# The causal mask of the diagonal attention blocks: an add into the kept row F on GpSimd and VectorE in place of small TensorE matmuls

## The chip, the cores and the metric

The kernel runs on one core of a Trainium2 chip. The metric is the device time of one execution in microseconds (us), as the median of several runs. A core has five engines that each work through their own instructions in order and wait for one another through semaphores: TensorE (PE in the profile; its weight loads are PEld), VectorE (DVE), ScalarE (ACT), GpSimd (POOL) and SyncE (SP, here a DMA queue). "SBUF" is the on-chip memory of 128 partitions, "PSUM" the accumulator memory that TensorE writes.

## What is computed

One decoder layer on 1024 tokens of width 1024: RMSNorm, one combined projection, a Mamba-2 (SSD) branch, a forgetting-attention branch (16 heads of 64), a gated merge, an output projection, and a post-norm with the residual. The change is in the attention branch alone:

```python
log_f = jax.nn.log_sigmoid(f_raw + fgate_b)        # one forget gate per head and token
fcum  = jnp.cumsum(log_f, axis=-1)                 # F
for blk in range(seqlen // 128):                   # 8 query blocks of 128
    s = q[q0:q1] @ k[:q1].T * scale + fcum[q0:q1, None] - fcum[None, :q1]
    s = jnp.where(kpos[None, :] <= qpos[:, None], s, -inf)
    o = softmax(s) @ v[:q1]
```

The mask matters only in the 128 x 128 square where a query block meets its own keys. Everything to the left of that square is allowed, and nothing to the right of it is computed.

## The kernel before

**The stages.** All large projections go through one stream of Strassen-like products (`Stream`, `Pair`), each a run of 12 matmuls of 128 x 512 in fp32r in two halves of 6 (`matmuls`, called through `mm`, L130). Their weights are split into a high and a low part by ScalarE (`wop<-raw` or `wop<-sum`, L351) and VectorE (L352). Their results leave PSUM through ScalarE (`s<-pb`, L404; `th<-pb`, L412) and VectorE (L414 to L418). From 0 to about 688 us this stream runs beside the SSD branch, from 688 to 1140 us beside attention, and after that alone.

**Attention.** Two heads are worked at a time, one on partitions 0 to 63 and one on 64 to 127, which makes 8 head pairs (`hp`). A pair has six groups, numbered here by `m` = 6 `hp` + `g` from 0 to 47. `GROUPS` (query blocks, half of the keys) is ((7,6),1), ((7,6),0), ((5,4),1), ((5,4),0), ((3,2),0), ((1,0),0). Within a group, `u` = 0 is the first named block and `u` = 1 the second. Groups g = 0, 2, 4 and 5 hold a diagonal square for both blocks, g = 1 and 3 hold none. So there are 32 groups with diagonal squares and 64 diagonal blocks for a pair of heads. The widths of the keys are 512 and 384 in g = 0 and 4, and 256 and 128 in g = 2 and 5.

**One group**, in program order:

- `scores`: for `u` = 0 and then 1, six fp32r matmuls (`s<-k,q`) and, in a diagonal block, four small bf16 matmuls (`s<-far,eye`) that add the mask into the last 128 columns. Then for each head VectorE adds the row F (tile `fb`, which is F of all keys, spread over 128 partitions) and takes the minimum (`ex<-s,fb`, L1464, a custom operation with a second instruction that reads its accumulator into `nm`), and ScalarE takes the exponential in place (`ex<-ex,nm`, L1468). A group so has four of each.
- `fill(m, 0)`: a planned share of matmuls of the stream, to keep TensorE at work while VectorE and ScalarE make the exponentials.
- `turned`: TensorE transposes the exponentials (`pt<-ident,ex`, L133). In even `m` other than 0 a small transpose of `ns` goes first, and the bank of the last key block, where only `u` = 0 takes part. The bank after that takes both heads of `u` = 0 and then both heads of `u` = 1. ScalarE, and for one bank VectorE, copies the banks out (`p<-pt`, L1499, L1497); ScalarE also sends a normalizer (`st<-pt`, L1391).
- `fill(m, 1)`, and then, at the start of the next round, `weighted`: the products with v (`av<-p,v`).

**What sets the order.** TensorE's order is that of the program (`keep_in_program_order`). So is that of everything wrapped in `pin`. The other instructions of VectorE, ScalarE, GpSimd and SyncE are ordered by the compiler's own scheduler, which may put an instruction of the stream between two of attention's. What each engine executes is then a fixed list.

**The mask before.** `eye` holds two shifted unit matrices and `far` the value 1e30 above the diagonal. For each head the two matmuls `eye` x `far` (64 rows each) add 1e30 where a key is later than the query. The sign is turned in the exponential (scale -1), so that 1e30 gives 0.

**Other users of the queues.** GpSimd carries the differences of the SSD operands (`less`, L213) with their stores (`t_s`, `t_a`, L195), the stores of attention's result (`ya_dram`, L1530) and of `ms_dram` (L1061), and in the last pair the sums of weights (L357, L373). SyncE issues nearly all loads, those of `fb` (L1333) among them: half 1 of the next pair in g = 2, half 0 in g = 5.

Of the kernel before, what the change touches and what calls it, by code (L numbers as in the profile page):

```python
# [16 lines left out]
P = 128  # L17
# [69 lines left out]
def hybrid_layer(ctx: ExitStack, tc, a, out):  # L87
# [41 lines left out]
    def mm(*args, **kw):  # L129
        return tc.keep_in_program_order(nc.tensor.matmul(*args, **kw))  # L130
# [7 lines left out]
    def small(name="th"):  # L138
        return gp.tile([P, HALF], F32, tag="th", name=name)
# [1153 lines left out]
    with tc.tile_pool(name="att", bufs=1, reuse_waits="tile", side="right") as ap, tc.tile_pool(  # L1293
# [1 line left out]
    ) as pp:  # L1295
        rows = [slice(64 * e, 64 * e + 64) for e in range(2)]

        eye = ap.tile([P, 192], BF16, name="eye")
        far = ap.tile([P, 192], BF16, name="far")
        nc.vector.memset(eye, 0.0)  # L1300
        big, beyond = small("big"), small("beyond")
        nc.vector.memset(big[:, 0:192], -NEG)
        for e in range(2):
            nc.vector.tensor_copy(eye[rows[e], 64:P], ident[rows[e], rows[e]])
            nc.gpsimd.affine_select(
                beyond[:, 192 * e : 192 * e + 192], big[:, 0:192], [[1, 192]], ALU.is_gt, 0.0, base=64 * e - 64,
                channel_multiplier=-1,
            )
            nc.vector.tensor_copy(far[rows[e], :], beyond[rows[e], 192 * e : 192 * e + 192])

        corner = [(eye[:, 64:192], far[:, 64:192]), (eye[:, 0:P], far[:, 0:P])]

# [123 lines left out]
        def scores(hp, g, u):  # L1436

            pair, h = GROUPS[g]
            i = pair[u]
            w = min(HALF, (i + 1) * P - h * HALF)  # L1440
            s = [pp.tile([P, HALF], F32, tag="s", bufs=4, name="s") for e in range(2)]
            t, keys = q[hp, pair], k[hp, h]
            isl = slice(i % 2 * P, i % 2 * P + P)
            ops = [(t[:, x, isl], keys[:, y, 0:w]) for x, y in ((0, 0), (0, 1), (1, 0))]
            diagonal = h == i // 4
            for m, (x, y) in enumerate(ops):
                for e in range(2):
                    mm(
                        s[e][:, 0:w], x[rows[e]], y[rows[e]], start=(m == 0), stop=(m == 2 and not diagonal),
                        skip_group_check=True,  # L1450
                    )
            if diagonal:
                for n, (x, y) in enumerate(corner):
                    for e in range(2):
                        mm(
                            s[e][:, w - P : w], x[rows[e]], y[rows[e]], start=False, stop=(n == 1),
                            skip_group_check=True,
                        )
            hd = heads[hp]
            for e in range(2):  # L1460
                o = ex[:, e, u, 0:w]
                nm = hd.at(hd.nm, i, h, e)
                pin(
                    nc.vector.tensor_tensor_reduce(  # L1464
                        o, s[e][:, 0:w], fb[hp, h][:, e, 0:w], 1.0, 3.0e38, ALU.add, ALU.min, nm
                    )
                )
                pin(nc.scalar.activation(o, o, AF.Exp, scale=-1.0, bias=nm, accum_out=hd.at(hd.sm, i, h, e)))  # L1468
# [258 lines left out]
```

## Time and profile before

| | us |
|---|---|
| median of 3 runs | 1303.09 (1302.53 to 1304.8) |
| the profiled execution | 1300.96 |
| its span, first to last instruction | 1299.3 |
| TensorE busy | 1256.0 |
| VectorE busy | 1005.9 |
| ScalarE busy | 792.0 |
| GpSimd busy | 262.0 |

The profile is of one execution. It gives each engine's instructions with start and duration, and for idle time before an instruction what ended it. The granted TensorE clock is 0.997 of full speed on average. Times below are us from the start of the span. In a row of a timeline the first number is the start, the second how long the row's instructions took together, and "xN" how many instructions of one kind are merged in it.

### The profile page before, as it was taken

Reading aid. Unit: us, or ns where it says so; the run is one execution under the profiler, and the core shown is the slowest. Engines: PE = TensorE matmul, PEld = TensorE weight load, DVE = VectorE, ACT = ScalarE, POOL = GpSimd, SP = SyncE. Lnnn points to the kernel's source line nnn. Section 1 sums busy time; section 2 is a strip of 40 time slices with the busy share of each in tenths; the row PEclk is TensorE's granted clock in tenths of the full one; section 3 lists DMA queues with packets and bytes.
Section 4 is the critical chain, followed back from the end, with each engine's and each line's share of the span. In section 5 each row is a group of like instructions: output and inputs, shape, how many; then the busy total and the mean of one; then the engine's idle time right before and its main releaser. Section 6 shows DMA issues by size and latency. Waiting matters only on the chain.

```text
span 1299.3 us, 20943 instructions
## 1 busy us (share of the span) xinstructions
PE 1256.0 (97%) x7054; PEld 984.4 (76%) x7054; DVE 1005.9 (77%) x1994; ACT 792.0 (61%) x1738; POOL 262.0 (20%) x250
## 2 busy tenths in 40 slices
PE   5999999999999999999999999999999999899997
PEld 4678778887888888878877777777667777678886
DVE  7989886987888888898676666666787677686975
ACT  7745665566665665566546566566775566653754
POOL 3000440012400340124001121120001001146052
PEclk9999999999999999999999999999999999999999
DMA  8233542645436543655375575666866658556932
GB/s 295 76 107 76 159 146 87 201 145 180 127 120 200 182 131 98 211 167 145 98 229 189 181 232 187 220 222 205 284 225 224 224 184 292 192 181 196 361 112 99
DMA packets 153515, 233.57 MB, mean 180 GB/s; under 512 B 15968, under 2 KB 61504, under 8 KB 153408
## 3 DMA queue, kind: packets, MB, share of 16 engines
q1 hardware_dynamic: 137408, 197.14, 47.7%
q10 hardware_dynamic: 11136, 19.11, 3.9%
q0 software_dynamic: 4864, 15.99, 3.2%
q8 instruction: 55, 0.90, 0.3%
q14 instruction: 52, 0.43, 0.1%
HBM read 162.99 MB, written 72.34 MB: 181 GB/s over the span
## 4 chain that ended last, share of the span: by engine, by line
PE 67%; DVE 12%; ACT 8%; DMA 7%; issue 4%; SPq 1%; POOL 0%; ACTq 0%; DVEq 0%; POOLq 0%
PE pb L130 28%; PE pc L130 15%; PE pd L130 5%; PE av L130 4%; PE pt L133 4%; PE s L130 4%; ACT ex L1468 3%; PE yps L130 2%; DVE wop L352 2%; ACT wop L351 1%; DVE sum L357 1%; DVE xs L771 1%; DVE ex L1464 1%; PE tr L133 1%; DMA xt<-in_x 1%
## 5 line engine op out<-in xcount | busy, mean ns | idle before, releaser
L1468 ACT ACTIVATE ex<-ex,nm 128x512 f32<-128x512 f32 (+1 forms) x192 | 116.0, 606 | 127.9 <-DVE nm L1464 127.8
L352 DVE TENSOR_TENSOR wop<-sum,wop 128x512 fp32r<-128x512 f32 x180 | 136.6, 760 | 56.4 <-ACT wop L351 54.8
L351 ACT ACTIVATE wop<-sum 128x512 fp32r<-128x512 f32 x180 | 112.3, 625 | 84.5 <-DVE sum L357 37.9
L404 ACT ACTIVATE s<-pb 128x512 f32<-128x512 f32 x144 | 85.1, 591 | 94.1 <-PE pb L130 90.9
L352 DVE TENSOR_TENSOR wop<-raw,wop 128x512 fp32r<-128x512 f32 x144 | 102.1, 710 | 45.2 <-ACT wop L351 43.9
L130 PE MATMUL pc<-x3h,wop 128*128 128x512 f32 x384 | 130.5, 397 | 1.7 <-DVE th L414 1.3
L130 PE MATMUL pb<-x0h,wop 128*128 128x512 f32 x384 | 131.2, 398 | 0.0
L130 PE MATMUL pb<-x5h,wop 128*128 128x512 f32 x384 | 129.3, 396 | 1.2 <-ACT s L404 1.2
L130 PE MATMUL pb<-x6h,wop 128*128 128x512 f32 x384 | 129.2, 395 | 1.3 <-ACT s L404 1.3
L130 PE MATMUL pc<-x2h,wop 128*128 128x512 f32 x384 | 130.2, 398 | 0.0
L130 PE MATMUL pb<-x4h,wop 128*128 128x512 f32 x384 | 129.4, 395 | 0.0
L1464 DVE CUSTOM_DVE_ANT_0 ex<-s,fb 128x512 f32<-128x512 f32 (+1 forms) x192 | 95.7, 552 | 34.1 <-PE s L130 34.0
L351 ACT ACTIVATE wop<-raw 128x512 fp32r<-128x512 f32 x144 | 89.6, 623 | 13.9 <-PE pd L130 6.1
L130 PE MATMUL pd<-x1h,wop 128*128 128x512 f32 x288 | 96.3, 394 | 0.0
L130 PEld LDWEIGHTS pc<-x3h,wop 128*128 128x128 f32 x384 | 72.4, 189 | 19.4 <-DVE th L414 1.7
L130 PEld LDWEIGHTS pb<-x5h,wop 128*128 128x128 f32 x384 | 72.1, 188 | 18.8 <-ACT s L404 2.3
L130 PEld LDWEIGHTS pb<-x6h,wop 128*128 128x128 f32 x384 | 72.2, 188 | 17.6 <-ACT s L404 1.7
L130 PEld LDWEIGHTS pc<-x2h,wop 128*128 128x128 f32 x384 | 72.1, 188 | 17.0 <-issue 1.4
L130 PEld LDWEIGHTS pb<-x0h,wop 128*128 128x128 f32 x384 | 72.7, 189 | 16.1 <-issue 0.9
L130 PEld LDWEIGHTS pb<-x4h,wop 128*128 128x128 f32 x384 | 72.1, 188 | 16.1 <-issue 0.9
L133 PE MATMUL pt<-ident,ex 128*128 128x128 f32 x576 | 77.2, 277 | 7.2 <-ACT ex L1468 6.7
L133 PEld LDWEIGHTS pt<-ident,ex 128*128 128x128 f32 x576 | 65.9, 142 | 19.4 <-ACT ex L1468 13.5
(310 smaller groups left out, 2918.8 us busy)
## 6 DMA issues: line engine op xcount, KB each, us to landing
raw<-in_wu SPq DMA_DIRECT2D x128, 256.0 KB
csb<-cs_dram SPq DMA_DIRECT2D x32, 256.0 KB
fb<-f_dram SPq DMA_DIRECT2D x16, 512.0 KB
rb<-st_dram SPq DMA_DIRECT2D x48, 128.0 KB
wd<-in_wo SPq DMA_DIRECT2D x40, 128.0 KB
xt<-in_x SPq DMA_DIRECT2D x8, 512.0 KB
gs_dram<-th ACTq DMA_DIRECT2D x16, 256.0 KB
qh_dram<-th ACTq DMA_DIRECT2D x16, 256.0 KB
```

What stands on the lines that cost most here:

```text
L130: return tc.keep_in_program_order(nc.tensor.matmul(*args, **kw))
L133: return tc.keep_in_program_order(nc.tensor.transpose(out_, in_, idn))
L351: nc.scalar.activation(op[:, 0], src, AF.Copy)
L352: nc.vector.tensor_tensor(op[:, 1], src, op[:, 0], ALU.subtract)
L357: self.adds.tensor_tensor(t, x, y, ALU.add)
L404: nc.scalar.activation(s, ps, AF.Copy)
L771: nc.vector.scalar_tensor_tensor(d, u[:, o + j : o + j + HALF], cw[:, tile_idx, j : j + 1], d, ALU.mult, ALU.add)
L1464: nc.vector.tensor_tensor_reduce(o, s[e][:, 0:w], fb[hp, h][:, e, 0:w], 1.0, 3.0e38, ALU.add, ALU.min, nm)
L1468: pin(nc.scalar.activation(o, o, AF.Exp, scale=-1.0, bias=nm, accum_out=hd.at(hd.sm, i, h, e)))
```

## The change

`eye`, `far` and the four small matmuls of each diagonal block are gone. One tile `beyond` (128 x 128, fp32) holds 1e30 above the diagonal. Before a diagonal block is reduced on VectorE, `beyond` is added in place to the 128 columns of `fb` that belong to its square, for both heads in one instruction (128 x 2 x 128). Columns of `fb` are masked only after the last block that needs them unmasked, so each of these adds also waits for earlier readers. Of the eight blocks of a head pair the odd ones (7, 5, 3, 1) are masked by GpSimd, a group or more ahead, and the even ones (6, 4, 2, 0, which are `u` = 1) by VectorE, between the two reductions of `u` = 0 and the two of `u` = 1. That makes 32 adds on GpSimd and 32 on VectorE; 256 matmuls and their 256 weight loads leave TensorE. The adds are pinned, so that they keep their place among the other pinned instructions of their engine.

```diff
-        eye = ap.tile([P, 192], BF16, name="eye")
-        far = ap.tile([P, 192], BF16, name="far")
...
-        corner = [(eye[:, 64:192], far[:, 64:192]), (eye[:, 0:P], far[:, 0:P])]
+        beyond = ap.tile([P, P], F32, name="beyond")
+        big = small("big")
+        nc.vector.memset(big[:, 0:P], -NEG)
+        nc.gpsimd.affine_select(beyond, big[:, 0:P], [[1, P]], ALU.is_gt, 0.0, base=0, channel_multiplier=-1)
...
+        def corner(hp, i, engine):
+
+            f = fb[hp, i // 4][:, :, i % 4 * P : i % 4 * P + P]
+            pin(engine.tensor_tensor(f, f, beyond.unsqueeze(1).to_broadcast([P, 2, P]), ALU.add))
...
             for m, (x, y) in enumerate(ops):
                 for e in range(2):
                     mm(
-                        s[e][:, 0:w], x[rows[e]], y[rows[e]], start=(m == 0), stop=(m == 2 and not diagonal),
-                        skip_group_check=True,
+                        s[e][:, 0:w], x[rows[e]], y[rows[e]], start=(m == 0), stop=(m == 2), skip_group_check=True,
                     )
-            if diagonal:
-                for n, (x, y) in enumerate(corner):
-                    for e in range(2):
-                        mm(
-                            s[e][:, w - P : w], x[rows[e]], y[rows[e]], start=False, stop=(n == 1),
-                            skip_group_check=True,
-                        )
             hd = heads[hp]
+            if u and h == i // 4:
+                corner(hp, i, nc.vector)
...
             hp, g = divmod(m, 6)
             more = hp + 1 < NK
+            if g in (1, 3, 4):
+                corner(hp, {1: 5, 3: 3, 4: 1}[g], nc.gpsimd)
+            if g == 4 and more:
+                corner(hp + 1, 7, nc.gpsimd)
...
+        corner(0, 7, nc.gpsimd)
```

More of the change, by code (lines that the diff above doesn't have):

```diff
@@ L1296, in hybrid_layer @@
         rows = [slice(64 * e, 64 * e + 64) for e in range(2)]
-        eye = ap.tile([P, 192], BF16, name="eye")
-        far = ap.tile([P, 192], BF16, name="far")
-        nc.vector.memset(eye, 0.0)
-        big, beyond = small("big"), small("beyond")
-        nc.vector.memset(big[:, 0:192], -NEG)
-        for e in range(2):
[L1304 to L1307, printed above, removed]
-            )
-            nc.vector.tensor_copy(far[rows[e], :], beyond[rows[e], 192 * e : 192 * e + 192])
-        corner = [(eye[:, 64:192], far[:, 64:192]), (eye[:, 0:P], far[:, 0:P])]
+        beyond = ap.tile([P, P], F32, name="beyond")
+        big = small("big")
+        nc.vector.memset(big[:, 0:P], -NEG)
+        nc.gpsimd.affine_select(beyond, big[:, 0:P], [[1, P]], ALU.is_gt, 0.0, base=0, channel_multiplier=-1)
         GROUPS = [((7, 6), 1), ((7, 6), 0), ((5, 4), 1), ((5, 4), 0), ((3, 2), 0), ((1, 0), 0)]
@@ L1444, in scores @@
             ops = [(t[:, x, isl], keys[:, y, 0:w]) for x, y in ((0, 0), (0, 1), (1, 0))]
-            diagonal = h == i // 4
             for m, (x, y) in enumerate(ops):
@@ L1448, in scores @@
                     mm(
-                        s[e][:, 0:w], x[rows[e]], y[rows[e]], start=(m == 0), stop=(m == 2 and not diagonal),
-                        skip_group_check=True,
-                    )
-            if diagonal:
-                for n, (x, y) in enumerate(corner):
-                    for e in range(2):
-                        mm(
-                            s[e][:, w - P : w], x[rows[e]], y[rows[e]], start=False, stop=(n == 1),
-                            skip_group_check=True,
-                        )
+                        s[e][:, 0:w], x[rows[e]], y[rows[e]], start=(m == 0), stop=(m == 2), skip_group_check=True,
+                    )
             hd = heads[hp]
+            if u and h == i // 4:
+                corner(hp, i, nc.vector)
             for e in range(2):
```

## The prediction

> **What bounds the kernel now.** I read the page's busy times and its chain first, then the table of stages, then TensorE's waits in the attention stage (688 to 1140 us), where the whole change lies.
>
> ```profile
> PE 1256.0 (97%) x7054; PEld 984.4 (76%) x7054; DVE 1005.9 (77%) x1994; ACT 792.0 (61%) x1738; POOL 262.0 (20%) x250
> ...
> PE 67%; DVE 12%; ACT 8%; DMA 7%; issue 4%; SPq 1%; POOL 0%; ACTq 0%; DVEq 0%; POOLq 0%
> ```
> ```profile
> 688.00:910.00 222.00, 221.21 (x1499) 168.63 (x1499) 147.34 (x398) 138.52 (x351) 36.09 (x41) 1.00 0.62 201
> 910.00:1140.00 230.00, 218.69 (x1508) 159.35 (x1506) 171.41 (x458) 151.24 (x394) 23.91 (x38) 0.99 0.68 229
> ```
> ```profile
> PE pt L133 <- ACT ex L1468: 6.7, 17, 1.3
> PE av L130 <- ACT p L1499: 4.5, 8, 1.2
> ```
>
> Until 910 us (pairs 0 to 3) TensorE is busy 221.21 of 222.00 us: an instruction taken from it there is time gained, if nothing else becomes late. From 910 to 1140 it idles 11.3 of 230 us, and those gaps name ScalarE: transposes wait for exponentials (6.7 us in 17 waits), products with v for copies (4.5 us in 8). There the chain scores, VectorE's reduction, ScalarE's exponential, transpose has no cover left.
>
> **What TensorE gets back.** One group with diagonal squares (pair 4, widths 512 and 384), and the next one, without:
>
> ```profile
> 919.34 0.98 PE L130 MATMUL s<-k,q 64*128 64x512 f32 x6
> 920.16 0.29 PE L130 MATMUL s<-far,eye 64*128 64x128 bf16 x4
> 920.26 0.77 PE L130 MATMUL s<-k,q 64*128 64x384 f32 x6
> 920.87 0.28 PE L130 MATMUL s<-far,eye 64*128 64x128 bf16 x4
> 921.09 0.50 PE L130 MATMUL pb<-x5h,wop 128*128 128x512 f32 x1
> ```
> ```profile
> 930.51 1.67 PE L130 MATMUL s<-k,q 64*128 64x512 f32 x12
> 932.11 0.50 PE L130 MATMUL pc<-x3h,wop 128*128 128x512 f32 x1
> ```
>
> Matmuls overlap, so I go by starts. The mask delays what follows it by 0.10 us in block `u` = 0 (920.16 to 920.26) and by 0.22 in `u` = 1 (920.87 to 921.09), of which some 0.1 is the switch to full-width matmuls that stays: at least 0.22 a group. From above: the unmasked group takes 1.60 us from first score to fill, the masked one 1.75, though its second block is narrower by 0.82 - 0.61 = 0.21: at most 0.36. I take **0.27**, inside both, for all 32 groups: 8.6 us (7.0 to 11.5) if every group of TensorE's queue became that much shorter. The compiled order shows TensorE's list otherwise unchanged, 512 entries fewer, so that the change does what it says there.
>
> It counts only where ScalarE is ready for an earlier TensorE. By the table below, 18 of the 32 groups have that: **18 x 0.27 = 4.9 us gained**.
>
> **What VectorE gets.** An add on two SBUF operands, 128 x 256 in all, between the reductions of `u` = 0 and `u` = 1. It must wait for the last reader of its columns, and the next reduction for it, both on VectorE itself.
>
> ```profile
> L1430 DVE TENSOR_TENSOR zr<-o 128x256 f32<-128x256 f32 x16 | 7.8, 487 | 0.1
> ```
> ```profile
> 915.58 0.20 DVE L1373 RECIPROCAL sm<-sm 128x8 f32<-128x8 f32 x1 [1.16 <-ACT ex L1468]
> 915.82 0.17 DVE L1374 TENSOR_SCALAR ns<-sm 128x8 f32<-128x8 f32 x1
> ...
> 923.40 0.69 DVE L1464 CUSTOM_DVE_ANT_0 ex<-s,fb 128x512 f32<-128x512 f32 x1
> 924.01 0.08 DVE L1464 DVE_READ_ACCUMULATOR2_ANT nm<- 128x1 f32 x1
> 924.01 0.55 DVE L1464 CUSTOM_DVE_ANT_0 ex<-s,fb 128x384 f32<-128x384 f32 x1
> ```
>
> Independent reductions overlap by 0.08 us (923.40 + 0.69 against 924.01). A dependent instruction starts 0.04 after the end of the one before (915.78, 915.82). So an add costs 0.12 + 0.49 + 0.04 = about 0.6 us, 19 us in 32. VectorE is 66 to 75% busy in these stages, and ScalarE, with exponentials 0.70 us apart, hides more than half: the third exponential of this group would be ready 0.3 us later than now. That alone costs little (below nothing too: the scores of `u` = 0 end 0.1 us earlier).
>
> **What the scheduler does with it.** This is the larger part. It now expects the exponentials of `u` = 1 late and puts stream work before them. In 14 groups, 13 of them of widths 512 and 384, ScalarE's compiled order has changed between the second exponential and the fourth. Pair 0, g = 0, and pair 4, g = 0:
>
> ```
> before    ex ex ex ex  s<-pb  wop  ...
> after  0  ex ex  s<-pb  wop  ex ex
> after  4  ex ex  s<-pb  wop  ex  st  p<-pt  ex
> ```
>
> ScalarE works in order, so the fourth exponential is later by what now stands ahead of it. The same pattern stands once in the kernel before, in pair 7, g = 4:
>
> ```profile
> 692.99 0.72 ACT L1468 ACTIVATE ex<-ex,nm 128x512 f32<-128x512 f32 x1 [1.37 <-DVE nm L1464]
> ...
> 694.41 0.60 ACT L1468 ACTIVATE ex<-ex,nm 128x384 f32<-128x384 f32 x1
> ...
> 695.01 0.60 ACT L1468 ACTIVATE ex<-ex,nm 128x384 f32<-128x384 f32 x1
> ...
> 695.62 0.58 ACT L404 ACTIVATE s<-pb 128x512 f32<-128x512 f32 x1
> 696.09 0.62 ACT L351 ACTIVATE wop<-raw 128x512 fp32r<-128x512 f32 x1
> 696.61 0.58 ACT L1499 ACTIVATE p<-pt 128x512 f32<-128x512 f32 x1
> ```
> ```profile
> 695.22 1.96 PE L133 MATMUL pt<-ident,ex 128*128 128x128 f32 x14
> ```
> ```profile
> 1128.90 0.57 ACT L412 ACTIVATE th<-pb 128x512 f32<-128x512 f32 x1
> 1129.38 0.61 ACT L351 ACTIVATE wop<-raw 128x512 fp32r<-128x512 f32 x1
> 1129.89 0.60 ACT L1468 ACTIVATE ex<-ex,nm 128x384 f32<-128x384 f32 x1
> ```
> ```profile
> 1130.64 2.18 PE L133 MATMUL pt<-ident,ex 128*128 128x128 f32 x9 [1.27 <-ACT ex L1468]
> ```
>
> The eviction holds ScalarE for 0.47 us (695.62 to 696.09), the weight's high part for 0.52: together 1.0. In pair 0, g = 0, TensorE's transposes already start (695.22) before the fourth exponential ends (695.61), so the 1.0 us goes straight onto the path; what moved ahead is no longer in the way of the copies, but those wait for the transposes, and TensorE's 6 fill matmuls and the products follow them. In pair 7, g = 4, the pattern is seen at work: the fourth exponential starts at 1129.89 and TensorE has idled 1.27 us for it.
>
> Done so for every affected group, with these intervals, for the start of its transposes and the end of its fill, the price is: pair 0, g = 0, 1.0; pair 1, g = 0, 0.2; pair 4, g = 0, 1.4 (`st` and a copy of a bank too); pair 4, g = 2, 1.0 (VectorE now runs a `wop`, two operand splits, the add and a copy between its reductions); pair 4, g = 4, 0.4; pair 5, g = 0, 0.8; pair 6, g = 4, 0.3; pair 7, g = 0, 0.6; pair 7, g = 4, 0.5. Nine groups, **6.2 us lost**. Five more groups (g = 4 of pairs 0 to 3, and pair 6, g = 0) have 18 matmuls of fill before the transposes and swallow it, two of them with all their gain. The rest of the 32, where nothing is gained or lost, are g = 5 of pairs 4, 5 and 7. Bounds of this term: 2 (only the two largest) to 9 (the full 1.0 or 1.4 wherever the order changed without cover).
>
> Some is given back. One wait of TensorE for a copy comes just behind the largest loss, and ScalarE does the work that causes it while TensorE stands:
>
> ```profile
> 938.95 1.95 PE L130 MATMUL av<-p,v 128*64 128x256 f32 x16 [0.69 <-ACT p L1499]
> ```
>
> I count **0.7 back** (0 to 2).
>
> **What GpSimd gets.** 32 adds of 128 x 256 with a broadcast operand:
>
> ```profile
> L872 POOL TENSOR_TENSOR xe<-xdt,tend 128x256 f32<-128x256 f32 x28 | 25.1, 895 | 216.1 <-DVE xdt L840 216.1
> ```
> ```profile
> 1094.40 1.32 POOL L357 TENSOR_TENSOR sum<-sum,raw 128x512 f32<-128x512 f32 x1 [0.63 <-DVE wop L352]
> ```
> ```profile
> 1093.88 2.39 DVE L278 SCALAR_TENSOR_TENSOR x4l<-x4l,x4h 128x512 fp32r<-128x512 f32 x2
> ```
>
> 0.9 us each is 29 us on an engine that is busy 60 of 452 us. But two VectorE instructions of 0.69 took 2.39 us while GpSimd ran one of its own: the second waited for GpSimd's end. GpSimd's adds for blocks 3 and 1 start right behind a group's last reduction, where VectorE wants to split weights. At most 32 x 0.9 = 29 us fall on VectorE; TensorE sees them only where VectorE has no slack (pairs 4 to 7), and I put **0.8 us** on the path (0 to 3). [...]
>
> Queued behind GpSimd's waiting adds are stores, of differences and of attention's result:
>
> ```profile
> 787.82 0.56 POOL L195 DMA_DIRECT2D t_s<-x  x1 [0.30 <-POOL x L213]
> ```
> ```profile
> 790.44 0.55 DVE L1464 CUSTOM_DVE_ANT_0 ex<-s,fb 128x384 f32<-128x384 f32 x1
> ```
>
> This store (pair 1) now stands behind the add for block 1, which waits for the reduction that ends at 790.99, and one more add: 790.99 + 2 x 0.9 = 792.8, 5 us late. A SyncE load of the next difference needs the store, but in the compiled order it has moved behind the loads of q and of weights. I cost the queues at nothing; a load that still waited behind it could cost up to those 5 us.
>
> **Sum.** -4.9 + 6.2 - 0.7 + 0.8 = +1.4. On the profiled execution's 1300.96 us that is 1302.4. The median of the runs shown, 1303.09, lies 2.1 above that execution, so the forecast for a median is **1304.5 us**, 0.1% slower: a loss of sign but hardly of size. About 0.2% (2.6 us) is what a measurement of this kernel can tell from no change.
>
> **Rivals.**
>
> - *The cover holds: faster.* ScalarE's moved work fills time in which it now idles for reductions, and only the two largest losses remain (2.4 us), while 25 groups gain: -6.8 + 2.4 = -4.4, 1298.7 us. For it: TensorE is 99.6% busy until 910 us. Against it: pair 7, g = 4, and the 17 waits for exponentials.
> - *The clock falls: slower.* Decides where a new stall follows idle time closely, as in pair 4, g = 0 and 2.
>
> ```profile
> 1127.00:1130.00 3.00, 1.37 (x6) 0.58 (x5) 1.90 (x7) 3.00 (x9) 0.00 (x0) 1.00 0.70 251
> 1130.00:1132.00 2.00, 1.36 (x7) 1.36 (x8) 1.66 (x4) 2.00 (x7) 0.54 (x1) 0.53 0.60 235
> 1132.00:1134.00 2.00, 2.00 (x9) 1.72 (x8) 0.43 (x1) 1.52 (x4) 0.00 (x0) 0.62 0.12 47
> ```
>
>   After 3 us with TensorE busy 1.37, its granted clock is 0.53 and 0.62 for 4 us: 0.47 x 2 + 0.38 x 2 = 1.7 us lost. Two more such places add 3.4: 1307.9 us. [...]
> - *GpSimd's adds come late: slower.* In the last pair the add for block 3 stands behind a sum that waits for VectorE:
>
> ```profile
> 1119.40 1.65 POOL L373 TENSOR_TENSOR sum<-sum,raw 128x512 f32<-128x512 f32 x1 [7.03 <-DVE wop L352]
> ```
>
>   It ends at 1121.05, the add at about 1122, and the first exponential of that block starts at 1126.87: 4 us of room. All other adds have more, but if VectorE splits that weight later, attention's end moves with it: 3 to 4 us, 1308 us.
>
> **How the numbers follow.** Forecast 0.45, with its own range 1302 to 1308 (its upper half beyond 0.2%); the cover holds 0.30; the clock 0.15; late adds 0.10. Faster 0.30; within 0.2% about half of the forecast's case, 0.23; slower 0.22 + 0.25 = 0.47. The range of 8 in 10 goes from most of the first rival's to the unknown ends of the others: 1297.5 to 1311.
>
> **What would show it.** Right: scores to fill shorter by 0.22 to 0.36 us in all 32 groups; VectorE's add 0.4 to 0.5 us with 0.1 of gap ahead; ScalarE's evictions between the exponentials; TensorE's wait for exponentials up from 6.7 to about 12 us, most of it in pairs 0, 4 and 5. Wrong: that wait unchanged (then the first rival), a granted clock below 1 between 920 and 1000 us (the second), or a reduction that waits for GpSimd (the third).

## The result, and the profile after

| | before | after |
|---|---|---|
| median, us | 1303.94 (1302.53 to 1306.66, 4 runs) | 1315.42 (1314.14 to 1316.41, 4 runs) |
| the profiled execution's span, us | 1299.3 | 1314.7 |

The changed kernel is 0.9% slower: a ratio of 1.0093, with a 95% interval of 1.0069 to 1.0117. That is 11.5 us, where +1.4 was forecast, and 1315.4 lies beyond the end of the range (1311).

Busy times and the chain's shares by engine, from the page of after:

```profile
PE 1258.9 (96%) x6798; PEld 985.0 (75%) x6798; DVE 1032.4 (79%) x2021; ACT 794.5 (60%) x1738; POOL 284.3 (22%) x281
...
PE 64%; DVE 13%; DMA 10%; ACT 7%; issue 4%; SPq 1%; POOL 0%; DVEq 0%; ACTq 0%; POOLq 0%
```

256 matmuls have gone, and yet TensorE's busy time has not fallen (1256.0 before). The table of stages says where (after the length come the busy us of PE, PEld, DVE, ACT and POOL, then TensorE's granted clock, DMA share and GB/s):

```profile
688.00:910.00 222.00, 219.33 (x1379) 166.25 (x1378) 161.47 (x411) 138.94 (x350) 47.37 (x57) 1.00 0.63 205
910.00:1152.00 242.00, 220.47 (x1369) 160.09 (x1368) 181.46 (x465) 151.68 (x387) 35.29 (x53) 0.96 0.66 218
```

The granted clock from 910 us on is 0.96, and was 0.99: some of TensorE's busy time is slow matmuls. Its waits over the attention stage (688 to 1152 us):

```profile
PE pt L133 <- ACT ex L1456: 19.3, 33, 2.0
PE av L130 <- ACT p L1487: 3.3, 6, 1.1
```

Transposes waited 6.7 us for exponentials before and 19.3 now. To see which groups, I took the starts of the first scores of all 48 groups from both traces. Attention is 13.1 us longer; of the other 2.3 us between the spans, 1.7 lie ahead of it (over all the traces here the first scores start anywhere from 686.6 to 691.2) and 0.6 behind. After's trace also has a stretch of half clock ahead of attention, from 316.2 us on, that before's does not have; the change does not touch that stage, and three of the later kernels' traces have the same stretch. The groups that changed by 0.4 us or more:

```
group             before   after - before
pair 0, g = 0      10.90   +0.52
pair 1, g = 0      10.75   +0.58
pair 3, g = 0      10.75   +0.41
pair 4, g = 0      11.17   +3.50    clock falls
pair 4, g = 2       7.71   +2.41    clock falls
pair 4, g = 4      10.29   +0.55
pair 5, g = 0      10.30   +2.52    clock falls
pair 6, g = 4       9.37   +0.49
pair 7, g = 0      10.15   +0.90
pair 7, g = 1      11.15   +2.67    clock falls
pair 7, g = 4      14.06   +1.17    clock falls (before too)
all groups that became shorter: -3.75, all that became longer: +16.86
```

**Pair 4, g = 0, in after.** TensorE, ScalarE and VectorE (timelines; brackets: idle time ahead and what ended it):

```profile
920.38 1.50 PE L130 MATMUL s<-k,q 64*128 64x512 f32 x12
921.81 0.50 PE L130 MATMUL pb<-x5h,wop 128*128 128x512 f32 x1
...
925.98 0.33 PE L133 MATMUL pt<-ident,ex 128*128 128x128 f32 x1 [1.05 <-ACT ex L1456]
926.69 0.55 PE L133 MATMUL pt<-ident,ex 128*128 128x128 f32 x3 [0.38 <-ACT ex L1456]
928.29 0.33 PE L133 MATMUL pt<-ident,ex 128*128 128x128 f32 x1 [1.05 <-ACT ex L1456]
929.30 1.20 PE L133 MATMUL pt<-ident,ex 128*128 128x128 f32 x9 [0.69 <-ACT ex L1456]
```
```profile
926.54 0.57 ACT L404 ACTIVATE s<-pb 128x512 f32<-128x512 f32 x1
927.02 0.61 ACT L351 ACTIVATE wop<-sum 128x512 fp32r<-128x512 f32 x1
927.54 0.60 ACT L1456 ACTIVATE ex<-ex,nm 128x384 f32<-128x384 f32 x1
...
928.29 0.36 ACT L1487 ACTIVATE p<-pt 128x256 f32<-128x256 f32 x1
928.56 0.60 ACT L1456 ACTIVATE ex<-ex,nm 128x384 f32<-128x384 f32 x1
```
```profile
924.29 0.68 DVE L1452 CUSTOM_DVE_ANT_0 ex<-s,fb 128x512 f32<-128x512 f32 x1
...
925.02 0.43 DVE L1328 TENSOR_TENSOR fb<-fb,beyond 128x256 f32<-128x256 f32 x1
925.59 0.56 DVE L1452 CUSTOM_DVE_ANT_0 ex<-s,fb 128x384 f32<-128x384 f32 x1
```

Scores to fill take 1.43 us (920.38 to 921.81), 1.75 before: the 0.32 that TensorE was to get back. The add delays the third reduction by 0.69 (1.30 after the second one's start instead of 0.61). Then ScalarE does an eviction and a weight ahead of the third exponential and a copy ahead of the fourth: exactly the order that the prediction read from the compiled lists. TensorE idles 1.05 and 0.69 us for them.

**The granted clock.** The same table in slices of 3.41 us, cut where the clock falls and rises again: three of after's five places in attention, a slice without a fall, and before's only place there.

```profile
927.09:930.50 3.41, 1.67 (x13) 1.34 (x12) 2.47 (x4) 2.16 (x8) 0.35 (x1) 1.00 1.05 406
930.50:933.91 3.41, 3.41 (x13) 2.04 (x13) 0.30 (x1) 1.09 (x2) 0.00 (x0) 0.51 0.82 314
947.59:951.00 3.41, 1.41 (x7) 0.53 (x5) 3.41 (x14) 1.44 (x6) 0.00 (x0) 1.00 0.38 135
951.00:954.41 3.41, 2.94 (x8) 2.11 (x8) 1.99 (x5) 2.32 (x7) 0.54 (x1) 0.50 0.32 100
...
1107.99:1111.40 3.41, 1.86 (x7) 0.79 (x5) 2.98 (x12) 2.63 (x7) 0.00 (x0) 1.00 0.96 258
1111.40:1114.81 3.41, 3.05 (x14) 3.06 (x15) 1.95 (x7) 2.97 (x8) 0.56 (x1) 0.51 0.74 274
...
923.68:927.09 3.41, 1.99 (x11) 1.14 (x9) 2.77 (x10) 1.97 (x6) 0.36 (x1) 1.00 1.02 377
```
```profile
1126.69:1130.10 3.41, 1.68 (x8) 0.67 (x6) 2.31 (x9) 3.23 (x9) 0.00 (x0) 1.00 0.64 228
1130.10:1133.51 3.41, 2.87 (x12) 2.68 (x13) 1.99 (x4) 3.41 (x9) 0.54 (x1) 0.50 0.40 156
```

Each fall here lasts 3.41 us at half the clock, which is 1.71 us of work lost. The falls of after start at multiples of 3.41 us from each other (930.5, 951.0, 991.9, 1111.4, 1145.5: 6, 18, 53 and 63 times 3.413), and in each slice ahead of one TensorE was busy 1.86 us or less of 3.41. With 1.99 (923.68) the clock stayed. In attention after has five, before one: four more are **6.8 us**.

**Pair 7, g = 1** has no add on VectorE and no new order on ScalarE, and is 2.67 us longer. Its place on VectorE and GpSimd in after:

```profile
1104.64 3.49 DVE L278 SCALAR_TENSOR_TENSOR x4l<-x4l,x4h 128x512 fp32r<-128x512 f32 x2
```
```profile
1104.97 0.75 POOL L1328 TENSOR_TENSOR fb<-fb,beyond 128x256 f32<-128x256 f32 x1
1105.66 1.30 POOL L357 TENSOR_TENSOR sum<-sum,raw 128x512 f32<-128x512 f32 x1
```

The two operand splits that took 2.39 us before take 3.49, to 1108.13, past the end of GpSimd's sum (1106.96), which now stands behind the new add. The first of the two alone runs from 1104.64 to 1107.53, until just behind the end of that sum. The first reduction, next on VectorE, comes 3.79 us after the group's start instead of 2.62, all four exponentials with it, and the clock falls.

### The profile page after: what moved, and what is told of

Read it like the earlier page. It is cut to its first block, busy times and chain, and to the rows that moved or that the text cites. A ratio compares the mean times of both kernels' runs of the same rounds, so it can differ in the third digit from the quotient of the medians.

```text
span 1314.7 us, 20568 instructions
## 1 busy us (share of the span) xinstructions
PE 1258.9 (96%) x6798; PEld 985.0 (75%) x6798; DVE 1032.4 (79%) x2021; ACT 794.5 (60%) x1738; POOL 284.3 (22%) x281
## 4 chain that ended last, share of the span: by engine, by line
PE 64%; DVE 13%; DMA 10%; ACT 7%; issue 4%; SPq 1%; POOL 0%; DVEq 0%; ACTq 0%; POOLq 0%
PE pb L130 27%; PE pc L130 15%; PE pd L130 5%; PE pt L133 4%; PE av L130 4%; PE s L130 3%; ACT ex L1456 3%; DVE wop L352 2%; PE yps L130 2%; DVE ex L1452 1%; DMA raw<-in_wu 1%; DMA fb<-f_dram 1%; ACT wop L351 1%; DVE sum L357 1%; DMA xr<-in_x 1%
## 5 line engine op out<-in xcount | busy, mean ns | idle before, releaser
L351 ACT ACTIVATE wop<-sum 128x512 fp32r<-128x512 f32 x180 | 112.2, 625 | 83.6 <-DVE sum L357 39.3
L404 ACT ACTIVATE s<-pb 128x512 f32<-128x512 f32 x144 | 85.1, 591 | 88.6 <-PE pb L130 84.3
L352 DVE TENSOR_TENSOR wop<-raw,wop 128x512 fp32r<-128x512 f32 x144 | 107.8, 750 | 34.0 <-ACT wop L351 33.9
L1452 DVE CUSTOM_DVE_ANT_0 ex<-s,fb 128x512 f32<-128x512 f32 (+1 forms) x192 | 98.4, 553 | 42.8 <-PE s L130 38.3
L133 PE MATMUL pt<-ident,ex 128*128 128x128 f32 x576 | 82.7, 283 | 20.2 <-ACT ex L1456 19.6
L351 ACT ACTIVATE wop<-raw 128x512 fp32r<-128x512 f32 x144 | 89.6, 623 | 12.7 <-PE pd L130 6.1
```

The costliest lines, as they stand in the source:

```text
L133: return tc.keep_in_program_order(nc.tensor.transpose(out_, in_, idn))
L351: nc.scalar.activation(op[:, 0], src, AF.Copy)
L352: nc.vector.tensor_tensor(op[:, 1], src, op[:, 0], ALU.subtract)
L404: nc.scalar.activation(s, ps, AF.Copy)
L1452: nc.vector.tensor_tensor_reduce(o, s[e][:, 0:w], fb[hp, h][:, e, 0:w], 1.0, 3.0e38, ALU.add, ALU.min, nm)
```

## The experiments

The theory after this reading (**order and clock**): the matmuls' time comes back as forecast; VectorE's add, and the order on ScalarE that it brings, make the exponentials late; and where TensorE's busy share of 3.41 us so sinks to about half, each wait costs another 1.71 us. Rivals: the **adds themselves**, whatever the order; **GpSimd** holding VectorE up. Two short edits recur. "Pins" keep the stream's ScalarE work of a group's first fill (the evictions of L404 and L412, the weights of L351) behind the four exponentials; the eviction is shown:

```diff
+                (pin if ATT else (lambda o: o))(nc.scalar.activation(s, ps, AF.Copy))
...
+            if g in (0, 2, 4):
+                ATT.append(1)
             fill(m, 0)
+            ATT.clear()
```

"Sum first" gives out one add of GpSimd later, so that in the compiled order it changes places with the sum:

```diff
-            if g in (1, 3, 4):
+            if g in ((1, 3, 4) if more else (3, 4)):
...
+            if m == 44:
+                corner(hp, 5, nc.gpsimd)
             for u in range(2):
                 scores(hp, g, u)
```

"Room for falls" is an estimate from a trace: slide a window of 3.41 us over TensorE's matmuls in the attention stage; the total length of the stretches in which it would be busy under 0.55 (from 0.56 on no full-clock slice of these traces was followed by a fall), divided by 3.41, is how many falls attention would have on average if the grid lay anywhere and every such window brought a fall. "Clock lost" needs no profile: each execution has its mean granted clock on record, and 1 less that clock, times the span, is averaged over all executions of a kernel. In every trace the clock is half over the last 2 to 5 us of the span, which is 1 to 3 us of it. All results, against before on the same chip:

```
run                    change from before, us   ratio (95% interval)      falls, room   clock lost, us
after                  +11.5                    1.0093 (1.0069, 1.0117)   5, 4.7        11.8
x1_no_adds              -4.2                    0.9971 (0.9957, 0.9984)   2, 1.7        5.1
x2_vectore_only         +7.1                    1.0053 (1.0033, 1.0072)   3, 4.0        8.5
x3_gpsimd_only          +0.6                    1.0004 (0.9991, 1.0017)   2, 1.9        8.2
x4_scalar_pinned        +4.2                    1.0035 (1.0022, 1.0049)   0, 1.0        3.3
x5_no_adds_pinned       -3.6                    0.9983 (0.9967, 0.9999)   2, 2.3        6.5
x6_two_copies           +2.2                    1.0016 (0.9999, 1.0033)   0, 1.3        6.1
x7_sum_first            +8.1                    1.0066 (1.0044, 1.0089)   6, 4.4        10.5
x8_selected_pins        -0.7                    0.9996 (0.9980, 1.0012)   0, 1.2        2.9
x9_fillers              +4.3                    1.0028 (1.0011, 1.0045)   0, 0          2.6
x10_half                -3.0                    0.9975 (0.9961, 0.9990)   1, 0.9        4.6
x11_selected_fillers    -1.2                    0.9991 (0.9975, 1.0007)   2, 1.2        3.6
```

Falls are half-clock slices in attention. Before itself has one in its trace, room for 0.5, and 4.4 us of clock lost (mean of 87 executions). In all, the profiles show 24 such slices, 20 of them the first at their place, where the rooms add up to 25. After loses 7.5 us more of clock than before over all its executions, so its profile is no exception. Among the executions of before, 1 us more of clock lost goes with 0.7 us more of time.

**No adds.** One line: the add in `corner` is not given out, so that the kernel leaves out the causal mask.

> The changed kernel with all 64 adds left out, so that the causal mask is not applied at all; the small matmuls are gone as in the change. This is TensorE's gain alone. Accounting from the trace of after: groups with cover are 0.27 to 0.32 us shorter. Scalar order theory (the loss comes from stream work that ScalarE does between the exponentials, and each long wait of TensorE is doubled by a fall of the granted clock): the compiled order of ScalarE is that of before again except in pair 4, g = 0, pair 6, g = 0, and pair 7, g = 4, so most groups gain: 4 to 7 us below before. Add theory (the add of 0.6 us on VectorE between the reductions is itself the loss) and GpSimd theory (its adds hold VectorE up) both expect the same here, 7 to 9 us below before. If it is not below before, TensorE's matmuls were no cost at all and all three fall.

Measured: 4.2 below, at the lower end of the 4 to 7 that the order theory gave. TensorE's gain is real: 0.25 to 0.33 us in most groups with diagonal squares, 7.7 us in all groups that became shorter. But pair 4, g = 0, is 3.3 us longer without any add. Its ScalarE:

```profile
920.85 0.60 ACT L1456 ACTIVATE ex<-ex,nm 128x384 f32<-128x384 f32 x1
...
921.45 0.58 ACT L404 ACTIVATE s<-pb 128x512 f32<-128x512 f32 x1
921.92 0.62 ACT L351 ACTIVATE wop<-sum 128x512 fp32r<-128x512 f32 x1
922.44 0.60 ACT L1456 ACTIVATE ex<-ex,nm 128x384 f32<-128x384 f32 x1
```

The scheduler puts an eviction and a weight ahead of the fourth exponential here as soon as TensorE's list is shorter: 1.0 us and a clock fall behind it make most of the 3.3. Taking the matmuls away already changes the order. Pair 7, g = 0, is 1.4 longer here too, though nothing new stands between its reductions or its exponentials; no run explains that.

**VectorE's adds only.** `corner` is called for the even blocks alone; the odd ones stay unmasked.

> The changed kernel without its 32 adds on GpSimd (odd query blocks are left unmasked); VectorE's adds stay. The compiled orders of ScalarE and VectorE are those of after, entry for entry. Scalar order theory: nearly all of the 11.5 us of after stays; only pair 7, g = 1, where two VectorE instructions took 3.49 us beside GpSimd's add and sum (2.39 before), gives its 2.7 us back: 8 to 9 us above before. Add theory: the same, 8 to 11 above. GpSimd theory: most of the loss goes, 0 to 3 above before or below it.

**GpSimd's adds only.** `corner` is called for the odd blocks alone; the even ones stay unmasked.

> The changed kernel without its 32 adds on VectorE (even query blocks are left unmasked); GpSimd's adds stay. ScalarE's compiled order is that of the kernel without any adds. Scalar order theory: 2 to 4 us below before (the gain of the kernel without adds, less 2.7 us for pair 7, g = 1). Add theory: the same, since the adds are gone too. GpSimd theory: most of the loss stays, 6 to 12 us above before.

Measured: +7.1 and +0.6. So VectorE's 32 adds with all they bring cost 11.3 us (7.1 against -4.2), GpSimd's 4.8 (0.6 against -4.2) or 4.4 (11.5 against 7.1). VectorE's side came out a little under the 8 to 9 us above that were expected; the GpSimd run missed its 2 to 4 us below, and GpSimd's share is larger than the one place in pair 7. With these adds 3.1 us more of clock are lost (8.2 against 5.1; 11.8 against 8.5 gives 3.3), though the trace of the GpSimd run has hardly more room for falls than that without adds. Where that comes from stays open.

**Pins, and pins without adds.**

> The whole change, all 64 adds in place, and in groups g = 0, 2 and 4 the stream's ScalarE work of the first fill (evictions and high parts of weights) is kept behind the group's four exponentials, so that ScalarE does them back to back in every group, as before the change. This run separates the order from the add. Scalar order theory: the waits of pair 4, g = 0 and 2, and pair 5, g = 0, go with their clock falls (8.4 us of them) and about 3 us of the smaller ones; pair 7, g = 1 stays: 1 us below to 3 above before. Add theory: VectorE still adds 0.6 us ahead of the third reduction in all 32 groups, and the loss stays: 8 us or more above before. A third way: the evictions now come late for TensorE's next use of their bank, and new waits for them (products of the stream that wait for s) take the place of the old.

> The changed kernel with no adds at all (no causal mask) and with the stream's ScalarE work kept behind the four exponentials in g = 0, 2 and 4: what the removal of the matmuls is worth when the order is held, and, against the pinned kernel that has the adds, what the adds cost when the order is held. Order theory: the kernel without adds was 4.2 us below before although pair 4, g = 0, lost 3.3 and pair 7, g = 0, 1.4; held back, these go: 7 to 9 us below before, no stretch with a granted clock below 1 but at most one, and the pinned kernel with adds (4.2 above) shows that the adds themselves cost 11 to 13 us, by later reductions and later copies. Pinning theory (holding the evictions back is what makes the copies late): this kernel is not faster than the one without adds and without pins, 2 to 5 us below before, and has the same 10 us of waits for copies as the pinned kernel with adds.

Holding the order takes 11.5 down to 4.2, no slice has a clock below 1, and pair 4, g = 0, goes from +3.50 to -0.67, pair 5, g = 0, from +2.52 to -0.99. But TensorE's waits with the pins and the adds, over the attention stage, are these:

```profile
PE av L130 <- ACT p L1489: 10.4, 13, 1.8
PE pt L133 <- ACT ex L1458: 9.6, 28, 0.7
```

Waits for copies went from 3.3 to 10.4 us: new waits, as in the expectation's third way, but of the products with v for copies. So 4.2 lies above the range of the order theory and below that of the adds. Without adds the pins bring nothing (-3.6 against -4.2), as the pinning theory expected: TensorE's waits for copies are 10.4 us there too, so that these come from the pins, and one of them, in pair 4, g = 2, lasts 3.5 us. Holding the order by force is not free, and with the order held the 64 adds still cost 7.8 us (4.2 against -3.6; some 5 to 10 by the two intervals). The adds themselves are a large part of the loss.

**A bare delay of 1.2 us in two groups of before.**

```diff
+            if u and (hp, g) in ((0, 0), (4, 0)):
+                idle = small('idle')
+                for n in range(2):
+                    pin(nc.scalar.activation(idle, fb[hp, h][:, n, :], AF.Copy))
```

> The kernel before, matmul mask and all, with only two ScalarE copies of 128 x 512 (1.0 us together) put between the second exponential and the third in two groups: pair 0, g = 0, where TensorE is otherwise busy without a gap, and pair 4, g = 0, where it waits 0.85 us already. Price by the order alone: both groups 1.0 us longer, or 0 to 1.0 in pair 0. Clock theory: pair 0, g = 0, is 0.5 to 1.0 longer with the granted clock at 1; pair 4, g = 0, 2.7 longer, 1.0 for the copies and 1.7 for four us at a clock of about half, with TensorE busy under half of the 3.4 us ahead of the fall. The whole kernel: 3 to 4 us above before with the fall, 1 to 2 without.

The pins of above are on in these two groups as well. In the order that was executed a weight (`wop`) of pair 0, and a weight and two operand copies (`x4h`) of pair 4, have so moved from ahead of the exponentials to behind them, and with them some of VectorE's work: the run is not the two copies alone. ScalarE in pair 0, g = 0, and TensorE in pair 4, g = 0, of this kernel:

```profile
696.42 1.28 ACT L1465 ACTIVATE idle<-fb 128x512 f32<-128x512 f32 x2
697.60 0.60 ACT L1474 ACTIVATE ex<-ex,nm 128x384 f32<-128x384 f32 x1
```
```profile
928.51 0.33 PE L133 MATMUL pt<-ident,ex 128*128 128x128 f32 x1 [0.84 <-ACT ex L1474]
929.22 0.55 PE L133 MATMUL pt<-ident,ex 128*128 128x128 f32 x3 [0.38 <-ACT ex L1474]
931.00 0.33 PE L133 MATMUL pt<-ident,ex 128*128 128x128 f32 x1 [1.24 <-ACT ex L1474]
...
935.06 1.30 PE L130 MATMUL av<-p,v 128*64 128x256 f32 x10 [0.86 <-ACT p L1505]
```

The whole kernel is 2.2 us above before, between the prices with and without a fall. Pair 0, g = 0, became 1.27 us longer for a delay of 1.18 (696.42 to 697.60): even where TensorE is otherwise always busy, a delay between the exponentials went onto the path in full, as the prediction priced this group. Pair 4, g = 0, became 2.75 longer, the number that was expected, for another reason: there was no fall, but the first exponential came 0.6 later as well, and a wait of 0.86 for a copy followed. And pair 7, g = 4, where before's trace has its fall, had none here and was 1.3 shorter. That spoke against the clock theory, and led to the grid: whether the clock falls would depend on where the fixed slices happen to cut a stretch of low use, so that one profile can miss it. By the author's estimate of where this trace's grid lies, its two slices at pair 4 (from 926.36 and 929.77) have 2.19 and 1.91 us of use, 0.64 and 0.56, while the 3.40 us from 926.90 have 1.65, 0.49, and the clock stayed at 1.00. In pair 4, g = 0, a window is under 0.55 over 2.5 us of positions, a chance of 2.5 / 3.41 = 0.73; at before's place over 1.7, a half.

**The sum first**, all else as in after.

> The whole change, but in the last pair GpSimd's add for block 5 is given out in g = 2 instead of g = 1: in the compiled order it changes places with the sum of weights ahead of it, and nothing else on any engine moves. In after, this sum ran after the add and held VectorE's split of an operand up (3.49 us for two instructions, 2.39 before), and the four exponentials of pair 7, g = 1, came 1.2 us late. Port theory: the two instructions take 2.4 us again, pair 7, g = 1, loses its 2.67 us, fall of the clock and all, and the kernel is 2.5 us below after (9 above before). If the exponentials were late for another reason, the group stays at 13.8 us and nothing is gained.

VectorE and GpSimd at the same place:

```profile
1100.84 2.38 DVE L278 SCALAR_TENSOR_TENSOR x4l<-x4l,x4h 128x512 fp32r<-128x512 f32 x2
```
```profile
1101.18 1.50 POOL L357 TENSOR_TENSOR sum<-sum,raw 128x512 f32<-128x512 f32 x1
```

The two splits are back at 2.38 us, and pair 7, g = 1, at +0.06 instead of +2.67. The whole kernel is 3.4 us better than after by the two differences, whose intervals overlap; the group decides. The cause that the expectation's first theory is named after is shown by no run. What the traces show is the order of the ends: the split beside GpSimd's sum ended behind it each time, at 1096.27 against 1095.72 in before, at 1107.53 against 1106.96 in after and at 1103.22 against 1102.68 here. An earlier start did not spare it: in after the split that was held started at 1104.64, ahead of the add (1104.97).

This execution also shows what a slow slice may bring after it (pair 4, g = 0), and a slice at the border:

```profile
919.59:923.00 3.41, 1.47 (x8) 0.59 (x6) 2.12 (x9) 2.36 (x6) 0.72 (x1) 1.00 1.01 380
923.00:926.41 3.41, 2.06 (x9) 1.77 (x10) 2.29 (x4) 1.77 (x7) 0.00 (x0) 0.50 1.05 405
926.41:929.82 3.41, 3.41 (x11) 2.34 (x11) 0.47 (x1) 1.09 (x2) 0.00 (x0) 0.50 0.69 265
967.38:970.79 3.41, 1.86 (x17) 1.53 (x15) 2.61 (x4) 3.41 (x10) 1.36 (x2) 1.00 0.00 1
970.79:974.20 3.41, 3.41 (x27) 2.27 (x27) 3.24 (x6) 3.09 (x8) 0.00 (x0) 1.00 0.06 22
```

The slice that was itself slow and held 2.06 us of slow matmuls (923.00) was followed by a second slow one (926.41), so that this place cost 3.41. Over all the traces a slow slice with up to 2.7 us of use was followed by another (four places), and one with 2.9 or more was not. And 1.86 us of use (967.38), as much as brought a fall in after, brought none here: these traces show no sharp border.

**Selected pins and the sum first.** The pins of above with `if m in (0, 6, 12, 18, 24, 26, 30, 46)`.

> The whole change with both mendings: ScalarE's stream work is kept behind the exponentials only in eight groups (g = 0 of pairs 0 to 5, g = 2 of pair 4, g = 4 of pair 7, where the trace of the fully pinned kernel is better than that of after), and the last pair's add for block 5 stands behind the sum. By the groups of the two traces: after's 13.1 us of attention less 0.6, 0.9, 0.3, 0.7, 4.2, 1.4, 3.5 and 2.0 in these groups and 2.7 in pair 7, g = 1: 3 us below before. Order theory: that, with a clock fall at most in one place. If copies become late in other groups, as in the fully pinned kernel, 0 to 4 above before. If adds cost by themselves what the fully pinned kernel suggests, it does not beat before by more than 0.2%.

Measured: 0.7 below, which is no difference that can be told. Pair 4, g = 0 is at +0.23 and pair 5, g = 0 at -0.99, as hoped; but pair 4, g = 2 keeps 1.05, pair 5, g = 1 is 1.12 longer, and pair 7, g = 0 keeps 0.89. The last case of the expectation holds.

**Idle transposes in the waits of after.** They are overwritten by the transposes that follow, and make no exponential come sooner.

```diff
+                        for _ in range(extra.pop((t, e), 0)):
+                            turn(bank[:, e, t, :], ident)
                         turn(bank[:, e, t, :], ex[:, e, 1 - t, b % 4 * P : b % 4 * P + P])
```

> The whole change, with idle transposes of the unit matrix put on TensorE where it waits for exponentials in six groups (pair 4, g = 0, 2 and 4, pair 5, g = 0, pair 7, g = 1 and 4): 6 to 20 a group, each into the place of a transpose that follows and overwrites it, 74 in all. They do no work and shorten no wait; they only keep TensorE busy. Clock theory: in the traces so far every half-clock stretch is one or two windows of 3.41 us on a fixed grid, and follows a window in which TensorE was busy 0.54 or less; after has room for 4.7 such windows in an execution (by the length of the stretches in which a window would be under 0.55), 1.71 us each. With the fillers no window is under 0.55, the granted clock is 1, and the kernel gets 5 to 8 us back: 3.5 to 6.5 above before. If the falls follow the waits and not TensorE's busy share, or cost nothing on the path, the time stays at 11 above before or grows by up to 3 us for the fillers themselves.

(The idle transposes are 86, not 74, and 6 to 23 a group.) TensorE from 910 us on, by the table of stages, and its waits over the whole stage:

```profile
910.00:1144.00 234.00, 221.66 (x1449) 162.86 (x1448) 180.46 (x463) 150.43 (x384) 35.26 (x53) 1.00 0.68 226
```
```profile
PE pt L133 <- ACT ex L1456: 10.1, 27, 0.9
PE av L130 <- ACT p L1492: 3.5, 6, 1.2
```

Work that does nothing makes the kernel 7.2 us faster (11.5 to 4.3 above before), and the clock is 1.00. The four groups with new falls become 1.2 to 1.5 us shorter each, and so does pair 7, g = 4. ScalarE, VectorE and GpSimd execute after's instructions in after's order, but for one exponential of pair 7, g = 4, which has moved ahead of a copy. The wait for exponentials is lower (19.3 to 10.1) because idle transposes fill it. This is the clock's share shown nearly by itself: 7.2 us, against 8.0 by the rooms (4.7 x 1.71) and 9.2 of clock lost (11.8 to 2.6).

**Half of the change.** Odd blocks by GpSimd's adds (the sum first), even blocks by TensorE, pins in pair 4, g = 0, and pair 7, g = 4.

```diff
+            if u and h == i // 4:
+                for e in range(2):
+                    mm(s[e][:, w - P : w], eye, beyond, start=False, stop=True, skip_group_check=True)
```

> Half of the change: the odd blocks are masked by GpSimd's adds as in the change (the last pair's add for block 5 behind the sum), the even blocks by TensorE, now with one bf16 matmul of 128 rows a head in place of two of 64 rows; VectorE's 32 adds are gone and no add stands between two reductions. ScalarE's stream work is kept behind the exponentials in pair 4, g = 0, and pair 7, g = 4. Theory so far: VectorE's add is what costs (by itself and by the order that it brings), GpSimd's adds about 1 to 2 us once the sum is first, TensorE's small matmuls of the even blocks 0.1 to 0.2 a group: 1 to 3 us below before, no new order of ScalarE. If GpSimd's adds cost what the run with these alone seemed to say (0.6 above before, 4.8 above the kernel without adds), it is 0 to 4 above before.

The row of its 64 matmuls (count, then busy us and mean ns), and its waits over the attention stage:

```profile
L130 PE MATMUL s<-beyond,eye 128*128 128x128 bf16 x64 | 9.3, 227 | 0.0
```
```profile
PE av L130 <- ACT p L1493: 7.3, 10, 1.8
PE pt L133 <- ACT ex L1462: 6.3, 19, 1.0
```

Measured: 3.0 below before (0.25%), with an interval of 1.3 to 5.1: **faster than both kernels**. Most groups of g = 0, 2 and 4 become 0.2 to 0.25 us shorter, little less than with all matmuls gone; pair 4, g = 0, is 1.4 longer in spite of its pins. No add stands between two reductions any more; other work of VectorE does in four groups, as in four of before. Four things differ from before at once: the odd blocks' adds, the cheaper matmul of the even blocks (from the mask's first matmul to the fill 0.10 us, 1119.74 to 1119.84, where the four small ones of before took 0.22), the pins in two groups and the sum's place. No run tells what each is worth; the cheaper matmul for all blocks, without any add, was not run.

**Selected pins with fillers.**

> The whole change with the pins in eight groups and the sum first (measured 0.7 us below before), and idle transposes in the three groups in which a window can still be busy less than 0.55 (pair 4, g = 2 and 4, pair 7, g = 4). Clock theory: that kernel has room for 1.2 falls an execution, 2.1 us; with the fillers none is left, 1 to 3 us below the kernel without fillers, 1.5 to 3.5 below before. If fillers only take TensorE's time: the same as it or up to 1 us more.

Measured: 1.2 below before and 0.5 below the kernel without fillers, too little to be told from nothing. Room for 1.2 falls is still there: in pair 7, g = 0, where no filler stands and the clock fell for two slices in this profile, and in pair 7, g = 4, where TensorE waits 1.83 us for a copy behind the fillers. The run is inconclusive.

## Why the prediction was wrong

By its own steps, in us of the two traces (attention +13.1):

- **What TensorE gets back: right for a group, too many groups.** 18 x 0.27 = 4.9 was forecast; fourteen groups became 0.12 to 0.32 shorter, 3.75 with the small ones. The run without adds has 7.7.
- **VectorE's add: its duration was right, its worth was not.** It took 0.43 us and put 0.69 on the third reduction, against 0.49 and 0.6. "That alone costs little" was wrong: with ScalarE's order held, the adds of both engines still cost 7.8 us.
- **The scheduler's order: right in most places, and its sum near, in part by luck.** Without the falls, the nine groups named lost 0.52, 0.58, 1.79, 0.70, 0.55, 0.81, 0.49, 0.90 and 1.17 (forecast 1.0, 0.2, 1.4, 1.0, 0.4, 0.8, 0.3, 0.6, 0.5): 7.5 us instead of 6.2, within its bounds. These losses hold the adds' own delay too. With ScalarE's order held, six of the nine groups lose theirs; pair 4, g = 2 and 4, and pair 7, g = 0, are still 1.0, 0.3 and 1.5 longer than before, and pair 7, g = 0, was 1.4 longer without any add.
- **0.7 given back**: TensorE's waits for copies fell from 4.8 to 3.3, but that is drowned in the groups above.
- **GpSimd: the hold-up right, the place not.** Its adds took 0.77 us, and weight splits on VectorE became slower in the mean, 0.75 us for 0.71, as these two rows of after (mean ns of one behind the busy us) and the one of before show:

```profile
L1328 POOL TENSOR_TENSOR fb<-fb,beyond 128x256 f32<-128x256 f32 x32 | 24.3, 767 | 89.4 <-DVE nm L1452 70.4 <-issue 11.6 <-DMA fb<-f_dram 7.3
...
L352 DVE TENSOR_TENSOR wop<-raw,wop 128x512 fp32r<-128x512 f32 x144 | 107.8, 750 | 34.0 <-ACT wop L351 33.9
```
```profile
L352 DVE TENSOR_TENSOR wop<-raw,wop 128x512 fp32r<-128x512 f32 x144 | 102.1, 710 | 45.2 <-ACT wop L351 43.9
```

  The 0.8 us on the path became 1.0 at one place (pair 7, g = 1), which was not seen, and a fall with it. The two rows that were quoted for this contention were that very place.
- **The clock: the step that failed.** The forecast's sum priced every new wait of TensorE at its own length and put the clock at nothing, though those waits fall into stretches where TensorE is already little used. The clock stood only among the rivals, with a chance of 0.15 and two new places; there were four, at 1.71 each, 6.8 us. The idle transposes gave 7.2 back, and over all executions after loses 7.5 more of clock than before. A mean clock of 0.99 over a stage looks harmless; the warning lies in how close single stretches of 3.41 us come to half use.

Together: -3.75 + 7.5 + 1.0 + 6.8, and 1.5 in six small groups that were not named, make 13.1. Without the 6.8 of the clock the sum would still have been 4.9 short: 1.3 of the order, 1.2 of TensorE's gain, 0.7 not given back, 0.2 of GpSimd, and the 1.5. Of the signs given, the wait for exponentials rose further than 12 us, and the clock below 1 between 920 and 1000 us was the one for the second rival. The sign of the change was the likeliest of the three, its size was off by a factor of eight. Not separated: by which waits the adds cost their 7.8 us under the pins (those for exponentials are 9.6 us with adds and 6.0 without, those for copies 10.4 in both), and what brings the lost clock in GpSimd's 4.4 to 4.8 us.

## What to carry to other kernels

Time taken from the bounding engine is lost again if the replacement stands in the chain that this engine waits for (here VectorE's adds: 11.3 us with all they bring, against 4.2 gained without adds). A replacement that can be done a stage ahead is the better candidate: the kernel that kept only those adds was 3.0 us faster than before, though with three other edits. Compare the compiled order group by group, on the engines that the change does not touch as well. And price a new wait of TensorE with the clock: its length, plus what a fall cost in these traces, 1.71 us of lost work, times the chance that a slice of 3.41 us around it has a use under 0.55, the share that the rooms above are counted with.

## What the hardware showed that was not expected

- The granted clock followed slices of 3.41 us on a grid that is fixed within an execution; the fall at the end of the span lies on the same grid (in before at 1293.95, 48 slices behind 1130.11; in after at 1312.85, 49 behind 1145.59). Over all 13 traces, the last 25 us left out: each of the 15 slices at full clock with TensorE busy under 0.46 of it was followed by a half-clock slice, of the 18 between 0.46 and 0.55 nine were, and of those from 0.56 on none (in the four traces without a fall in attention the place of the grid is the author's estimate). An example without a fall is the kernel with the pins, where TensorE was busy 1.58 us of 3.41 from 1134.29 on and the clock stayed. No idle slice was needed for a fall: in after one followed 1.86 us of use in 3.41 (from 1107.99).
- The grid's place differs between the traces (before's fall at 1130.11 and after's first in attention, at 930.55, are 58.5 slices apart), so that the same stall can cost 1.71 us in one execution and nothing in the next. One profile is one draw: the profile of before fell once in attention where its room is 0.5, that of the kernel with two copies not at all where its room is 1.3. The 87 executions of before have mean clocks from 0.993 to 0.999.
- 86 transposes that compute nothing made a kernel 7.2 us faster.
